# Layer 1 of a two-layer diffusion trunk: high and low weight products in longer groups, down products of two output tiles alternating

## The chip, the cores and the metric

One core of one Trainium2 chip runs the whole program. The metric is the device time of one execution in microseconds (us), the median of several. TensorE (PE) does the matrix products, VectorE (DVE), ScalarE (ACT) and GpSimd (POOL) work elementwise, and SyncE (SP) issues the weight loads.

## The reference

Two layers over 256 latent tokens (and 256 context tokens, which layer 1 only reads) of width 2048. Layer 0 mixes tokens by pooling, layer 1 by neighbourhood attention; each is followed by a gated FFN with a width-3 convolution over tokens. What the change touches is layer 1's output projection and FFN:

```python
D_MODEL, SEQ, D_FF = 2048, 256, 5504

def conv_ffn(u, w_gate, w_up, conv_w, conv_b, w_down):
    T = u.shape[1]
    gp = jnp.pad(u @ w_gate, ((0, 0), (1, 1), (0, 0)))
    gte = gp[:, :T] * conv_w[0] + gp[:, 1:T + 1] * conv_w[1] + gp[:, 2:] * conv_w[2] + conv_b
    return (jax.nn.silu(gte) * (u @ w_up)) @ w_down

# layer i, latent stream
h = h + ml[:, 2] * y_lat              # y_lat of attention ends in o @ w_o
h = h + ml[:, 5] * conv_ffn(modulate(rms_norm(h, norm2_g[i]), ml[:, 3], ml[:, 4]),
                            ffn_w_gate[i], ffn_w_up[i], ffn_conv_w[i], ffn_conv_b[i], ffn_w_down[i])
```

## The kernel before

All products are float32 products made of three shorter ones. A weight tile arrives in pieces of 128 x 1024; `split` (L175, L177) casts each to a high part on ACT, and subtracts it on DVE (of some pieces on POOL) to get the low part. Both parts go into buffers that rotate: six pieces in the FFN, three in the attention. Activations stand as [high | low], 2 x 256 columns. A 512-wide product with the high weight part gives high x high and high x low in the two halves of one PSUM bank; a 256-wide product with the low weight part is added to the second half. They are called high and low products here.

The FFN of layer 1 has 43 tiles of 128 hidden channels, `f`. `gu1(f)` makes a gate tile `g` and an up tile `u`, each over 16 slices `k` of the input: two weight pieces of eight slices. `part` (L1182) does, for one piece, eight high products (L1188) and then eight low ones (L1191), so a tile reads 8 high, 8 low, 8 high, 8 low. `gate1` turns the two banks into one activation tile: `eg` and `eu` join the halves (ACT L1201, DVE L1202), `g1b` is the convolution (ACT L1210, DVE L1211 and L1213), `sgb` the SiLU (ACT L1216) times `eu` (DVE L1217), and `actb` splits that into high and low (ACT L1219, DVE L1220).

Four `f` make a chunk. After the next chunk's tiles, `down1` multiplies a chunk's four activation tiles with 16 output tiles, in four groups `mg` of four (weights `wd_0` to `wd_3` by group). Each output tile takes four high products (L1241) and four low ones (L1245) into one bank; ACT takes the bank out as `dy` (L1255), and POOL adds it to the stream `hl` (L1257) in two halves. Four banks rotate here, so output tile 6 uses the bank of tile 2. There are eleven chunks; the last is done differently and stays so. The gate of the last `f` of the chunk in work is called behind output tile 1 (L1259), so its steps lie at the head of the down phase, among the evictions and the splits of `wd_3`. The o products of the attention (L1614, L1617) follow the scheme of the gate tiles.

A scheduler of the framework fixes, before the run, the order of the instructions on each engine; within an engine they start in that order. The names in a row of the order have counters at the end: `dy_3_2` is chunk 3's eviction of tile 2, `d_3_0_2` is its bank (chunk, group, tile in the group), and `wd_3_3h` is the high part of chunk 3's group 3 (wd_3h in the trace).

Of the kernel before, what the change touches and what calls it, by code (L numbers as in the profile page):

```python
# [17 lines left out]
P = 128  # L18
D = 2048
KT = D // P  # L20
T = 256
# [40 lines left out]
def kernel(ctx: ExitStack, tc: tile.TileContext, xT, cxT, wmod, wg, wu, wd, wp,  # L62
                         wq, wv, wo, vec, cc, rope, inv, strips, out):
    nc = tc.nc
# [8 lines left out]
    def bank(tag, name):  # L73

        if tag == "d" and nbank[0] is not None:
            nbank[0] += 1
            if nbank[0] % 4 == 0:
                tag = "m"
        return pp.tile([P, 512], F32, tag=tag, bufs={"gu": 4, "d": 3, "m": 1}[tag], name=name)

    def flat(a):
        return a.rearrange("p s t -> p (s t)")
# [5 lines left out]
    def V(name):  # L88
        a, b = _OFF[name]
        return vt[0][:, a:b] if b <= NFIRST else vt[1][:, a - NFIRST : b - NFIRST]  # L90
# [72 lines left out]
    def split(ts, name, share=0, keep=False):  # L163

        parts = []
        for j, (t, n) in enumerate(ts):
            turn[0] += 1
            pools = [whp] * 3 + extra
            pool = pools[turn[0] % len(pools)]
            hi = pool.tile([P, 1024], F32R, tag="wh", name=f"{name}h{j}")  # L170
            lo = pool.tile([P, 1024], F32R, tag="wl", name=f"{name}l{j}")
            with ExitStack() as behind:
                for ins in hold:
                    behind.enter_context(tc.issue_after(ins))
                casts.append(nc.scalar.copy(hi[:, :n], t[:, :n]).ins)  # L175
                eng = nc.gpsimd if share and turn[0] % share == 0 else nc.vector
                low_of[:] = [eng.tensor_tensor(lo[:, :n], t[:, :n], hi[:, :n].bitcast(F32), op=ALU.subtract).ins]  # L177
            parts.append((hi, lo))
        if not keep:
            used(ts)  # L180
        return parts

    def ld(src, name, share=0):
        return split(load(lambda a, b: src[:, a:b], 2048, name), name, share)
# [157 lines left out]
    def M(l, which, k, s):  # L342
        return modT[l, which * 4 + k // 4][:, k % 4, s : s + 1]
# [138 lines left out]
    with ExitStack() as ph0:  # L482
# [72 lines left out]
        acts = {}  # L555
# [3 lines left out]
        with ExitStack() as phs:  # L559
# [16 lines left out]
            for j in range(2):  # L576
                t = st.tile([P, 2, WP], F32, bufs=1, name=f"pad{j}")
# [8 lines left out]
            for j in range(2):  # L586
                t = st.tile([P, 4, 32], F32, bufs=1, name=f"sh{j}")
# [239 lines left out]
            for g in range(4):  # L827
# [4 lines left out]
                last = [14]  # L832
# [210 lines left out]
        parts = ld(wv[0, 0], "wv0_0")  # L1043
        normalise_by(h_of, [(k, 0) for k in (2, 3)], rstds, f0, -1)
        last = None
        for kk in range(4):
            for i in range(2):
                ins = first_values(parts, i, kk, last)
                if (kk, i) == (1, 1):
                    with tc.issue_after(ins):  # L1050
                        v1 = n3.sums_of(1)
                    last = n3.done
                if (kk, i) == (2, 1):
                    with tc.issue_after(ins):
                        rstds[1] = n3.spread(1, v1)
                    last = n3.done
# [33 lines left out]
    with ExitStack() as ph2:  # L1090
# [13 lines left out]
        B = {}  # L1104
# [63 lines left out]
        def gu1(f):  # L1168
            if f == 0:
                return first1()  # L1170
            if f == 3:
                hold.clear()
            parts, res = [], []
            for nm, wsrc in (("g", wg), ("u", wu)):
                if f == 1 and nm == "u":
                    hold[:] = [done_b[8][0], done_b[-1][1]]
                parts.append(ahead.pop() if ahead else ld(wsrc[1, f], f"w{nm}1_{f}", 2 if f % 4 > 1 else 0))
                res.append(bank("gu", f"{nm}1_{f}"))
            if f == 1:
                hold[:] = done_b[-1]  # L1180

            def part(q, j):  # L1182

                ps = res[q]
                hi, lo = parts[q][j]
                for k in range(8 * j, 8 * j + 8):
                    c = P * (k % 8)
                    nc.tensor.matmul(ps, hi[:, c : c + P], flat(B[k]), start=(k == 0), stop=False)  # L1188
                for k in range(8 * j, 8 * j + 8):
                    c = P * (k % 8)  # L1190
                    nc.tensor.matmul(ps[:, T:], lo[:, c : c + P], B[k][:, 0], start=False, stop=(k == KT - 1))  # L1191

            for q, j in ((0, 0), (1, 0), (0, 1), (1, 1)) if f == 1 else ((0, 0), (0, 1), (1, 0), (1, 1)):
                part(q, j)
            return res

        def gate1(f, banks):
# [27 lines left out]
        def down1(c, fs, acts, after=None):  # L1225
            n = len(fs)
            last = c == len(chunks) - 1
            for mg in range(4):
                parts = split(load(lambda a, b: wd[1, mg, :, fs[0] + a // 512 : fs[0] + b // 512, :], 512 * n, f"wd1_{c}_{mg}"),
                              f"wd1_{c}_{mg}")  # L1230
                for m in range(4):
                    ps = bank("d", f"d1_{c}_{mg}_{m}")
                    for i in range(n):
                        hi, lo = parts[i // 2]
                        o = 512 * (i % 2) + P * m
                        if last:
                            nc.tensor.matmul(ps[:, :T], hi[:, o : o + P], acts[i][:, 0], start=(i == 0), stop=False)
                            nc.tensor.matmul(ps[:, :T], hi[:, o : o + P], acts[i][:, 1], start=False, stop=False)
                            nc.tensor.matmul(ps[:, :T], lo[:, o : o + P], acts[i][:, 0], start=False, stop=(i == n - 1))
                            continue  # L1240
                        nc.tensor.matmul(ps, hi[:, o : o + P], flat(acts[i]), start=(i == 0), stop=False)  # L1241
                    for i in range(0 if last else n):
                        lo = parts[i // 2][1]
                        o = 512 * (i % 2) + P * m
                        nc.tensor.matmul(ps[:, T:], lo[:, o : o + P], acts[i][:, 0], start=False, stop=(i == n - 1))  # L1245
                    k = 4 * mg + m
                    if last:
                        nc.vector.scalar_tensor_tensor(hl[:, k, :], ps[:, :T], M(1, 5, k, 0), hl[:, k, :],
                                                       op0=ALU.mult, op1=ALU.add)
                        n5.add_stream(h_lat, k, 0, None, (KT - 2, KT - 1))  # L1250
                        for j in {KT - 2: (), KT - 1: (KT - 2, KT - 1)}.get(k, (k,)):
                            nc.scalar.activation(hl[:, j, :], hl[:, j, :], AF.Copy, scale=V("fg")[:, j : j + 1])
                    else:
                        y = f1.tile([P, 2, T], F32, tag="t2", name=f"dy1_{c}_{k}")
                        nc.scalar.activation(flat(y), ps, AF.Copy, scale=M(1, 5, k, 0))  # L1255
                        for q in range(2):
                            nc.gpsimd.tensor_tensor(hl[:, k, :], hl[:, k, :], y[:, q], op=ALU.add)  # L1257
                    if after is not None and 4 * mg + m == 1:
                        after()  # L1259

        prev = None
        for c, fs in enumerate(chunks):
            acts = []
# [45 lines left out]
def _attention(tc, ap0, bank, ld, load, split, used, A, M, hl, wq, wv, wo, rope, strips, ident, v_first, xs, aside, hold):  # L1309

    nc = tc.nc
# [7 lines left out]
    with ExitStack() as es:  # L1319
# [6 lines left out]
        for j in range(2):  # L1326
            t = op.tile([P, 10 * W], F32, name=f"strip{j}")
# [4 lines left out]
        for j in range(2):  # L1332
            t = op.tile([P, 2, T], F32R, name=f"qz{j}")
# [173 lines left out]
        X = {}  # L1507
# [9 lines left out]
        for g in range(4):  # L1517
            v = v_group(g)
            for j in range(4):
                m = 4 * g + j  # L1520
# [38 lines left out]
        for m in range(2):  # L1559
            hold[:] = latest[2] if m else copies  # L1560
            parts = ld(wo[m], f"wo{m}")
            hold.clear()
            ps = bank("gu", f"op{m}")
# [7 lines left out]
        t = third[0][0]  # L1571
# [19 lines left out]
        for m in range(KT):  # L1591
            if m < len(early):
                o_end(early[m][0], m)
                continue
            if m == 3:
                third = load(lambda a, b: wo[3][:, 1024 + a : 1024 + b], 1024, "wo3b")
                parts = [None] + split(third, "wo3b")
                for k in range(8, KT):
                    o_mm(p3, parts, k)
                o_end(p3, m)  # L1600
                continue
            hold[:] = latest[2] if m == 2 else ()
            parts = ld(wo[m], f"wo{m}")
            hold.clear()
            ps = bank("gu", f"op{m}")
            if m == KT - 1:
                for k in range(KT):
                    o_mm(ps, parts, k, True)
            else:
                for j in range(2):  # L1610
                    hi, lo = parts[j]
                    for k in range(8 * j, 8 * j + 8):
                        c = P * (k % 8)
                        nc.tensor.matmul(ps, hi[:, c : c + P], X[k].rearrange("p s t -> p (s t)"), start=(k == 0), stop=False)  # L1614
                    for k in range(8 * j, 8 * j + 8):
                        c = P * (k % 8)
                        nc.tensor.matmul(ps[:, T:], lo[:, c : c + P], X[k][:, 0], start=False, stop=(k == KT - 1))  # L1617
            ins = o_end(ps, m)
        return ins

# [98 lines left out]
```

## Time and profile before

| | us |
|---|---|
| median of 3 runs | 2998.61 (2997.27 to 2998.90) |
| the profiled execution, its own time | 2999.81 |
| its span in the trace | 2998.03 |
| layer 1's FFN in the trace | about 2266 to 2983 |

Every time in a row is counted from the start of the span. In the table of stretches a row has the stretch, its length, and then for PE, PE's weight loads, DVE, ACT and POOL the busy time with the count of instructions, then the granted clock of TensorE, the share of the DMA engines and GB/s. In a timeline "x4" puts four instructions of a kind together from the first start to the last end; the number in brackets is the idle time before the row and what ended it. The granted clock 1.00 stands for 2.4 GHz, 0.50 for 1.2 GHz.

### The profile page before, as it was taken

What the parts mean: (1) busy time and instruction counts of PE and PEld (TensorE: products, weight loads), DVE (VectorE), ACT (ScalarE), POOL (GpSimd) and SP (SyncE); (2) the same over time, 40 slices, a digit from 0 to 9 for tenths busy, and PEclk for the clock granted to TensorE, in tenths of its full rate; (3) what the DMA queues carried; (4) which work ended last, traced back from release to release, by engine and by line L of the source; (5) the groups of instructions that cost most, each with busy time, mean ns of one, the idle gap of its engine ahead of it and who ended that gap; (6) DMA issues with size and microseconds to landing.
All of it is one profiled execution on the core that took longest, in us unless ns stands there. A gap on an engine that the chain in (4) does not pass through costs nothing.

```text
span 2998.0 us, 40831 instructions
## 1 busy us (share of the span) xinstructions
PE 2946.4 (98%) x15068; PEld 2410.7 (80%) x15068; DVE 1989.7 (66%) x2887; ACT 1378.9 (46%) x2239; POOL 808.8 (27%) x782
## 2 busy tenths in 40 slices
PE   5999999999999999999999999999999999999998
PEld 3666678888888888888888888888788888888887
DVE  5465799757484766748576657484868666666666
ACT  4333564333333243332335534353556666666665
POOL 0000006212203031220314002020003665666665
PEclk9999999999999999999999999999999999999999
DMA  9988554566574847557472334343355555555553
GB/s 395 343 314 302 204 180 157 191 202 191 169 230 141 258 138 221 181 177 229 144 252 83 121 107 129 100 131 106 115 166 201 183 190 195 189 183 183 186 193 113
DMA packets 178935, 561.80 MB, mean 187 GB/s; under 512 B 17712, under 2 KB 22576, under 8 KB 178736
## 3 DMA queue, kind: packets, MB, share of 16 engines
q1 hardware_dynamic: 178736, 559.19, 56.2%
q8 instruction: 119, 1.95, 0.2%
q14 instruction: 80, 0.66, 0.1%
HBM read 557.03 MB, written 2.10 MB: 186 GB/s over the span
## 4 chain that ended last, share of the span: by engine, by line
PE 90%; DMA 4%; DVE 3%; POOL 1%; issue 1%; ACT 1%; SPq 0%; DVEq 0%; ACTq 0%; POOLq 0%
PE g L1188 5%; PE u L1188 5%; PE d L971 5%; PE d L969 5%; PE d L970 5%; PE d L1241 5%; PE g L906 4%; PE g L904 4%; PE g L905 4%; PE u L906 4%; PE u L904 4%; PE u L905 4%; PE g L1191 3%; PE u L1191 3%; PE d L1245 2%; PE k L1373 2%
## 5 line engine op out<-in xcount | busy, mean ns | idle before, releaser
L317 DVE SCALAR_TENSOR_TENSOR macc<-wm,sc,macc 128x512 f32<-128x512 f32 (+1 forms) x420 | 379.5, 937 | 70.6 <-DMA wm<-wmod 69.5
L983 POOL TENSOR_TENSOR hl<-hl,dy 128x256 f32<-128x256 f32 x160 | 158.2, 989 | 984.3 <-ACT dy L982 984.2
L1257 POOL TENSOR_TENSOR hl<-hl,dy 128x256 f32<-128x256 f32 x320 | 323.3, 1045 | 214.6 <-ACT dy L1255 212.4
L982 ACT ACTIVATE dy<-d,modT 128x256 f32<-128x256 f32 x320 | 133.4, 470 | 193.0 <-PE d L971 176.4
L983 POOL TENSOR_TENSOR hc<-hc,dy 128x256 f32<-128x256 f32 x160 | 130.7, 817 | 0.0
L1255 ACT ACTIVATE dy<-d,modT 128x512 f32<-128x512 f32 x160 | 104.4, 683 | 43.4 <-PE d L1245 41.9
L177 DVE TENSOR_TENSOR wd_2l<-wd,wd_2h 128x1024 fp32r<-128x1024 f32 (+1 forms) x44 | 56.0, 1277 | 91.3 <-ACT wd_2h L175 90.3
L177 DVE TENSOR_TENSOR wd_3l<-wd,wd_3h 128x1024 fp32r<-128x1024 f32 (+1 forms) x44 | 53.8, 1242 | 79.8 <-ACT wd_3h L175 78.6
L249 PE MATMUL mod<-wm,sc 128*32 128x512 f32 x704 | 86.3, 625 | 6.5 <-DMA wm<-wmod 5.0
L1343 POOL TENSOR_TENSOR rk<-rk,rp 128x256 f32<-128x256 f32 x16 | 12.3, 771 | 296.0 <-DVE rk L1342 296.0
L177 DVE TENSOR_TENSOR wd_1l<-wd,wd_1h 128x1024 fp32r<-128x1024 f32 (+1 forms) x44 | 54.8, 1249 | 48.5 <-ACT wd_1h L175 48.5
L413 POOL TENSOR_TENSOR n2v<-n2v,minus_half 128x4 f32<-128x4 f32 x1 | 1.0, 1012 | 308.8 <-DVE n2v L412 308.8
L175 ACT CAST wd_1h<-wd 128x1024 fp32r<-128x1024 f32 (+1 forms) x44 | 45.3, 1031 | 67.7 <-PE u L905 41.6
L1440 ACT ACTIVATE sb<-sb,nm 128x512 f32<-128x512 f32 x64 | 46.1, 721 | 58.9 <-DVE nm L1436 40.3
L538 ACT ACTIVATE sg<-g 128x512 f32<-128x512 f32 x43 | 27.2, 632 | 99.7 <-DVE g L535 99.7
L177 DVE TENSOR_TENSOR wd_0l<-wd,wd_0h 128x1024 fp32r<-128x1024 f32 (+1 forms) x44 | 54.6, 1246 | 24.9 <-ACT wd_0h L175 24.9
L969 PE MATMUL d<-act,wd_1h 128*128 128x512 f32 x172 | 67.0, 390 | 0.8 <-ACT dy L982 0.8
L969 PE MATMUL d<-act,wd_2h 128*128 128x512 f32 x172 | 67.0, 390 | 0.0
L970 PE MATMUL d<-act,wd_2h 128*128 128x512 f32 x172 | 66.9, 389 | 0.0
L970 PE MATMUL d<-act,wd_1h 128*128 128x512 f32 x172 | 66.9, 389 | 0.0
L969 PE MATMUL d<-act,wd_0h 128*128 128x512 f32 x172 | 66.9, 389 | 0.0
L971 PE MATMUL d<-act,wd_2l 128*128 128x512 f32 x172 | 66.7, 390 | 0.1
(1800 smaller groups left out, 9233.8 us busy)
## 6 DMA issues: line engine op xcount, KB each, us to landing
wm<-wmod SPq DMA_DIRECT2D x384, 512.0 KB, 6.3
wd<-wd SPq DMA_DIRECT2D x168, 512.0 KB, 4.3
wg<-wg SPq DMA_DIRECT2D x156, 512.0 KB, 4.7
wu<-wu SPq DMA_DIRECT2D x156, 512.0 KB, 4.7
wv<-wv SPq DMA_DIRECT2D x32, 512.0 KB, 3.8
wk<-wq SPq DMA_DIRECT2D x32, 512.0 KB, 3.7
wq<-wq SPq DMA_DIRECT2D x32, 512.0 KB, 3.6
wo<-wo SPq DMA_DIRECT2D x31, 512.0 KB, 4.5
```

What stands on the lines that cost most here:

```text
L177: low_of[:] = [eng.tensor_tensor(lo[:, :n], t[:, :n], hi[:, :n].bitcast(F32), op=ALU.subtract).ins]
L317: nc.vector.scalar_tensor_tensor(acc[s], v, sc2[:, k, s : s + 1], acc[s], op0=ALU.mult, op1=ALU.add)
L904: nc.tensor.matmul(ps, hi[:, c : c + P], xh, start=(k == 0), stop=False)
L905: nc.tensor.matmul(ps, hi[:, c : c + P], xl, start=False, stop=False)
L906: ins = nc.tensor.matmul(ps, lo[:, c : c + P], xh, start=False, stop=(k == KT - 1))
L969: nc.tensor.matmul(ps, hi[:, o : o + P], xh, start=(i == 0), stop=False)
L970: nc.tensor.matmul(ps, hi[:, o : o + P], xl, start=False, stop=False)
L971: ins = nc.tensor.matmul(ps, lo[:, o : o + P], xh, start=False, stop=(i == n - 1))
L983: nc.gpsimd.tensor_tensor(h_of(s)[:, k, :], h_of(s)[:, k, :], y[:, s], op=ALU.add)
L1188: nc.tensor.matmul(ps, hi[:, c : c + P], flat(B[k]), start=(k == 0), stop=False)
L1191: nc.tensor.matmul(ps[:, T:], lo[:, c : c + P], B[k][:, 0], start=False, stop=(k == KT - 1))
L1257: nc.gpsimd.tensor_tensor(hl[:, k, :], hl[:, k, :], y[:, q], op=ALU.add)
```

## The change

Three places of layer 1 are written in another order. A gate or up tile does all 16 high products and then all 16 low ones (82 tiles; the tiles of `f` = 0 and 1 stay as they are). The o products of output tiles 6 to 14 do the same (9 tiles). In the first ten chunks the output tiles of the down products go in pairs: four high of one, four high of the next, then the four low of one and the four low of the next, held behind the last high product (80 pairs). The number of instructions and their sizes stay.

```diff
--- before.py
+++ after.py
@@ -1179,19 +1179,19 @@
             if f == 1:
                 hold[:] = done_b[-1]
 
-            def part(q, j):
+            def part(q, js):
 
                 ps = res[q]
-                hi, lo = parts[q][j]
-                for k in range(8 * j, 8 * j + 8):
+                ks = range(8 * js[0], 8 * js[-1] + 8)
+                for k in ks:
                     c = P * (k % 8)
-                    nc.tensor.matmul(ps, hi[:, c : c + P], flat(B[k]), start=(k == 0), stop=False)
-                for k in range(8 * j, 8 * j + 8):
+                    nc.tensor.matmul(ps, parts[q][k // 8][0][:, c : c + P], flat(B[k]), start=(k == 0), stop=False)
+                for k in ks:
                     c = P * (k % 8)
-                    nc.tensor.matmul(ps[:, T:], lo[:, c : c + P], B[k][:, 0], start=False, stop=(k == KT - 1))
-
-            for q, j in ((0, 0), (1, 0), (0, 1), (1, 1)) if f == 1 else ((0, 0), (0, 1), (1, 0), (1, 1)):
-                part(q, j)
+                    nc.tensor.matmul(ps[:, T:], parts[q][k // 8][1][:, c : c + P], B[k][:, 0], start=False, stop=(k == KT - 1))
+
+            for q, js in ((0, (0,)), (1, (0,)), (0, (1,)), (1, (1,))) if f == 1 else ((0, (0, 1)), (1, (0, 1))):
+                part(q, js)
             return res
 
         def gate1(f, banks):
@@ -1228,21 +1228,33 @@
             for mg in range(4):
                 parts = split(load(lambda a, b: wd[1, mg, :, fs[0] + a // 512 : fs[0] + b // 512, :], 512 * n, f"wd1_{c}_{mg}"),
                               f"wd1_{c}_{mg}")
+                pair = {}
                 for m in range(4):
-                    ps = bank("d", f"d1_{c}_{mg}_{m}")
-                    for i in range(n):
+                    if last:
+                        ps = bank("d", f"d1_{c}_{mg}_{m}")
+                    elif m % 2 == 0:
+                        for mm in (m, m + 1):
+                            pair[mm] = bank("d", f"d1_{c}_{mg}_{mm}")
+                            for i in range(n):
+                                o = 512 * (i % 2) + P * mm
+                                high = nc.tensor.matmul(pair[mm], parts[i // 2][0][:, o : o + P], flat(acts[i]),
+                                                        start=(i == 0), stop=False)
+                        for mm in (m, m + 1):
+                            for i in range(n):
+                                o = 512 * (i % 2) + P * mm
+                                with ExitStack() as behind:
+                                    if i == 0:
+                                        behind.enter_context(tc.issue_after(high.ins))
+                                    nc.tensor.matmul(pair[mm][:, T:], parts[i // 2][1][:, o : o + P], acts[i][:, 0],
+                                                     start=False, stop=(i == n - 1))
+                    if not last:
+                        ps = pair[m]
+                    for i in range(n if last else 0):
                         hi, lo = parts[i // 2]
                         o = 512 * (i % 2) + P * m
-                        if last:
-                            nc.tensor.matmul(ps[:, :T], hi[:, o : o + P], acts[i][:, 0], start=(i == 0), stop=False)
-                            nc.tensor.matmul(ps[:, :T], hi[:, o : o + P], acts[i][:, 1], start=False, stop=False)
-                            nc.tensor.matmul(ps[:, :T], lo[:, o : o + P], acts[i][:, 0], start=False, stop=(i == n - 1))
-                            continue
-                        nc.tensor.matmul(ps, hi[:, o : o + P], flat(acts[i]), start=(i == 0), stop=False)
-                    for i in range(0 if last else n):
-                        lo = parts[i // 2][1]
-                        o = 512 * (i % 2) + P * m
-                        nc.tensor.matmul(ps[:, T:], lo[:, o : o + P], acts[i][:, 0], start=False, stop=(i == n - 1))
+                        nc.tensor.matmul(ps[:, :T], hi[:, o : o + P], acts[i][:, 0], start=(i == 0), stop=False)
+                        nc.tensor.matmul(ps[:, :T], hi[:, o : o + P], acts[i][:, 1], start=False, stop=False)
+                        nc.tensor.matmul(ps[:, :T], lo[:, o : o + P], acts[i][:, 0], start=False, stop=(i == n - 1))
                     k = 4 * mg + m
                     if last:
                         nc.vector.scalar_tensor_tensor(hl[:, k, :], ps[:, :T], M(1, 5, k, 0), hl[:, k, :],
@@ -1607,14 +1619,14 @@
                 for k in range(KT):
                     o_mm(ps, parts, k, True)
             else:
-                for j in range(2):
-                    hi, lo = parts[j]
-                    for k in range(8 * j, 8 * j + 8):
+                for js in ((0,), (1,)) if m < 6 else ((0, 1),):
+                    for k in range(8 * js[0], 8 * js[-1] + 8):
                         c = P * (k % 8)
-                        nc.tensor.matmul(ps, hi[:, c : c + P], X[k].rearrange("p s t -> p (s t)"), start=(k == 0), stop=False)
-                    for k in range(8 * j, 8 * j + 8):
+                        nc.tensor.matmul(ps, parts[k // 8][0][:, c : c + P], X[k].rearrange("p s t -> p (s t)"),
+                                         start=(k == 0), stop=False)
+                    for k in range(8 * js[0], 8 * js[-1] + 8):
                         c = P * (k % 8)
-                        nc.tensor.matmul(ps[:, T:], lo[:, c : c + P], X[k][:, 0], start=False, stop=(k == KT - 1))
+                        nc.tensor.matmul(ps[:, T:], parts[k // 8][1][:, c : c + P], X[k][:, 0], start=False, stop=(k == KT - 1))
             ins = o_end(ps, m)
         return ins
 
```

On PE, at the head of chunk 3's down phase, before, from the last high product of output tile 0:

```order
L1241 MATMUL d_3_0_0_21552<-actb_20911,wd_3_0h_21548 128x512
L1245 MATMUL d_3_0_0_21552<-actb_20555,wd_3_0l_21545 128x256
L1245 MATMUL d_3_0_0_21552<-actb_20661,wd_3_0l_21545 128x256
L1245 MATMUL d_3_0_0_21552<-actb_20767,wd_3_0l_21549 128x256
L1245 MATMUL d_3_0_0_21552<-actb_20911,wd_3_0l_21549 128x256
L1241 MATMUL d_3_0_1_21565<-actb_20555,wd_3_0h_21544 128x512
```

The same place in the changed kernel, where the high product is L1240 and the low one L1248:

```order
L1240 MATMUL d_3_0_0_21552<-actb_20911,wd_3_0h_21548 128x512
L1240 MATMUL d_3_0_1_21557<-actb_20555,wd_3_0h_21544 128x512
L1240 MATMUL d_3_0_1_21557<-actb_20661,wd_3_0h_21544 128x512
L1240 MATMUL d_3_0_1_21557<-actb_20767,wd_3_0h_21548 128x512
L1240 MATMUL d_3_0_1_21557<-actb_20911,wd_3_0h_21548 128x512
L1248 MATMUL d_3_0_0_21552<-actb_20555,wd_3_0l_21545 128x256
```

Four high products of tile 1 moved in front of the low products of tile 0.

The scheduler also moved instructions of other engines. ACT, the same down phase, before:

```order
L1255 ACTIVATE dy_3_1_21574<-d_3_0_1_21565,modT_20_11884 128x512
L1201 COPY eg_21578<-g_19_21462 128x256
L1201 COPY eu_21581<-u_19_21475 128x256
L1210 ACTIVATE g1b_21584<-eg_21578,vt_71 128x256
L175 CAST wd_3_3h_21752<-wd_3_3_0_21748 128x1024
L175 CAST wd_3_3h_21756<-wd_3_3_1024_21750 128x1024
L1216 ACTIVATE sgb_21588<-g1b_21584 128x256
L1255 ACTIVATE dy_3_2_21603<-d_3_0_2_21594,modT_20_11884 128x512
```

And ACT in the changed kernel:

```order
L1267 ACTIVATE dy_3_1_21574<-d_3_0_1_21557,modT_20_11884 128x512
L1201 COPY eg_21578<-g_19_21462 128x256
L1201 COPY eu_21581<-u_19_21475 128x256
L175 CAST wd_3_3h_21752<-wd_3_3_0_21748 128x1024
L1210 ACTIVATE g1b_21584<-eg_21578,vt_71 128x256
L175 CAST wd_3_3h_21756<-wd_3_3_1024_21750 128x1024
L1216 ACTIVATE sgb_21588<-g1b_21584 128x256
L1267 ACTIVATE dy_3_2_21612<-d_3_0_2_21594,modT_20_11884 128x512
```

The first cast of wd_3 and `g1b` changed places; `sgb` still stands before the eviction of tile 2, and those of tiles 3 to 5 follow it.

DVE at the same place, before:

```order
L1202 TENSOR_TENSOR eu_21581<-eu_21581,u_19_21475 128x256
L1211 SCALAR_TENSOR_TENSOR g1b_21584<-eg_21578,vt_71,g1b_21584 128x255
L1213 SCALAR_TENSOR_TENSOR g1b_21584<-eg_21578,vt_71,g1b_21584 128x255
L177 TENSOR_TENSOR wd_3_3l_21753<-wd_3_3_0_21748,wd_3_3h_21752 128x1024
L177 TENSOR_TENSOR wd_3_3l_21757<-wd_3_3_1024_21750,wd_3_3h_21756 128x1024
L1217 TENSOR_TENSOR sgb_21588<-sgb_21588,eu_21581 128x256
```

And DVE in the changed kernel:

```order
L1202 TENSOR_TENSOR eu_21581<-eu_21581,u_19_21475 128x256
L177 TENSOR_TENSOR wd_3_3l_21753<-wd_3_3_0_21748,wd_3_3h_21752 128x1024
L1211 SCALAR_TENSOR_TENSOR g1b_21584<-eg_21578,vt_71,g1b_21584 128x255
L177 TENSOR_TENSOR wd_3_3l_21757<-wd_3_3_1024_21750,wd_3_3h_21756 128x1024
L1213 SCALAR_TENSOR_TENSOR g1b_21584<-eg_21578,vt_71,g1b_21584 128x255
L1217 TENSOR_TENSOR sgb_21588<-sgb_21588,eu_21581 128x256
```

The two subtractions of wd_3 moved in front of the two convolution steps of `g1b`, one before each. The other nine down phases read the same on ACT and DVE.

## Rows read from the trace of the kernel before

**Rows 1.** The page: busy us of each engine, with its share of the span.

```profile
PE 2946.4 (98%) x15068; PEld 2410.7 (80%) x15068; DVE 1989.7 (66%) x2887; ACT 1378.9 (46%) x2239; POOL 808.8 (27%) x782
```

**Rows 2.** Stretches of layer 1's FFN: us, then busy us of each engine, clock.

```profile
2340.00:2943.00 603.00, 603.00 (x3452) 529.45 (x3451) 405.91 (x397) 371.23 (x538) 382.56 (x322) 1.00 0.57 188
2943.00:2982.80 39.80, 39.80 (x274) 36.97 (x274) 28.48 (x43) 30.32 (x58) 30.17 (x32) 1.00 0.19 60
```

**Rows 3.** The chain of waits, one gate tile: start us, us, what.

```profile
2294.41 1.84 PE g L1188 x8
2296.25 0.95 PE g L1191 x8
```

**Rows 4.** Timeline, PE: first and last product of long runs of one width.

```profile
1006.99 0.40 PE L904 MATMUL g<-A,wg_26h 128*128 128x512 f32 x1
...
1016.54 0.39 PE L904 MATMUL g<-A,wg_26h 128*128 128x512 f32 x1
...
2252.90 0.28 PE L1539 MATMUL op<-A,wo15h 128*128 128x256 f32 x1
...
2258.30 0.28 PE L1539 MATMUL op<-A,wo15h 128*128 128x256 f32 x1
```

**Rows 5.** Tile wg_20h, 2561 to 2580: shortest/median/longest ns, first and last start.

```profile
L1188 PE MATMUL g<-A,wg_20h x16: 387/395/398, 2567.0 to 2578.4; 128*128 128x512 f32 x16
L175 ACT CAST wg_20h<-wg x2: 1039/1044/1050, 2562.1 to 2563.1; 128x1024 fp32r<-128x1024 f32 x2
```

**Rows 6.** Timeline, head of chunk 3's down products (start us, us, engine, line).

```profile
2551.53 1.09 PE L1241 MATMUL d<-actb,wd_0h 128*128 128x512 f32 x4
...
2553.13 0.69 ACT L1255 ACTIVATE dy<-d,modT 128x512 f32<-128x512 f32 x1 [1.30 <-PE d L1245]
...
2554.54 0.69 ACT L1255 ACTIVATE dy<-d,modT 128x512 f32<-128x512 f32 x1 [0.72 <-PE d L1245]
...
2555.12 0.36 ACT L1201 COPY eg<-g 128x256 f32<-128x256 f32 x1
...
2555.37 0.39 ACT L1201 COPY eu<-u 128x256 f32<-128x256 f32 x1
...
2555.97 0.60 ACT L1210 ACTIVATE g1b<-eg,vt 128x256 f32<-128x256 f32 x1 [0.21 <-DVE eg L1202]
...
2556.48 1.99 ACT L175 CAST wd_3h<-wd 128x1024 fp32r<-128x1024 f32 x2
2556.61 0.65 DVE L1211 SCALAR_TENSOR_TENSOR g1b<-eg,vt,g1b 128x255 f32<-128x255 f32 x1 [0.34 <-ACT g1b L1210]
...
2557.30 0.48 DVE L1213 SCALAR_TENSOR_TENSOR g1b<-eg,vt,g1b 128x255 f32<-128x255 f32 x1
2557.70 2.35 DVE L177 TENSOR_TENSOR wd_3l<-wd,wd_3h 128x1024 fp32r<-128x1024 f32 x2
...
2558.37 0.42 ACT L1216 ACTIVATE sgb<-g1b 128x256 f32<-128x256 f32 x1
...
2558.69 2.40 ACT L1255 ACTIVATE dy<-d,modT 128x512 f32<-128x512 f32 x4
...
2559.95 1.09 PE L1241 MATMUL d<-actb,wd_1h 128*128 128x512 f32 x4
```

**Rows 7.** Timeline, the same place in chunk 8: third eviction and tile 6.

```profile
2894.39 2.39 ACT L1255 ACTIVATE dy<-d,modT 128x512 f32<-128x512 f32 x4
...
2895.65 1.09 PE L1241 MATMUL d<-actb,wd_1h 128*128 128x512 f32 x4
```

**Rows 8.** Groups by line, VectorE (DVE), 2340 to 2943: busy us, mean ns.

```profile
L1213 DVE SCALAR_TENSOR_TENSOR g1b<-eg,vt,g1b 128x255 f32<-128x255 f32 x36 | 37.8, 1049 | 1.3
...
L177 DVE TENSOR_TENSOR wd_3l<-wd,wd_3h 128x1024 fp32r<-128x1024 f32 x18 | 21.2, 1219 | 0.0
```

**Rows 9.** Two other stretches where PE pauses, with their granted clock (PEclk).

```profile
42.90:46.30 3.40, 2.64 (x16) 0.68 (x16) 3.03 (x7) 2.01 (x5) 0.00 (x0) 0.50 1.03 411
...
2262.00:2266.00 4.00, 3.52 (x25) 2.93 (x24) 2.33 (x5) 0.64 (x1) 3.17 (x3) 1.00 0.63 184
```

## The prediction

> **What bounds the kernel now.** I read the busy shares first: TensorE (PE) works 98% of the span, VectorE (DVE) 66%, ScalarE (ACT) 46% [rows 1]. A share is an average, so the stretch that the change touches comes next. In layer 1's FFN PE is busy 603.00 of 603.00 us, then 39.80 of 39.80, at a granted clock of 1.00 [rows 2]. Every product there starts as the one before it lets it, and nothing that another engine does shows in the end. So two things can move the time: the pace of PE through a reordered row of products, and a new moment at which another engine is too late for it. For the first I read PE's pace in runs of one width [rows 3, 4], for the second the handover of one down phase, engine by engine [rows 6]. The profiled execution took 2999.81 us, 1.20 above the median of 2998.61; differences are worked out inside the trace and put on the median.
>
> **PE's pace: a small gain.** Instruction counts stay. A gate or up tile is now 8 high products in 1.84 us, 8 low in 0.95, and both again [rows 3], 5.58 in all. Without a change of width a high product follows the last at (1016.54 - 1006.99)/42 = 0.2274 us, and a 256-wide one at (2258.30 - 2252.90)/45 = 0.1200 us (42 and 45 products of one width lie between the rows) [rows 4]. So 16 high take 1.84 + 8 x 0.2274 = 3.66, 16 low 0.95 + 8 x 0.12 = 1.91, together 5.57: 0.01 us less. That is 91 tiles (82 gate and up tiles, 9 o products), -0.9 us. A down tile takes (2559.95 - 2551.53)/6 = 1.403 us [rows 6]; a pair was 2.81 and becomes 1.403 + 4 x 0.2274 + 4 x 0.12 = 2.79, -0.014 each, and 80 pairs give -1.1. Sum **-2.0 us**; the starts are rounded to 0.01 us, so I keep 0 to -4. The same run of 256-wide products excludes that a longer row of low products starves on its weight loads: it holds 0.1200 over 45 [rows 4].
>
> A rule speaks against even this gain. The rows show that the change of width costs a little: 1.84/8 = 0.230 against 0.2274 [rows 3, 4]. The Trainium skill ("TensorE: Matmul & The Clock Gate", section "Back-to-back issue gap") gives the gap of an isolated product from its own width alone, N/2.4 + 2.5 ns, which is 215.8 ns at 512 and 109.2 at 256. By it the order of widths is worth nothing, and the sum would lose its -2.0. The trace is about 11 ns slower at either width, so I keep the rows.
>
> **The weights: nothing.** The second half's high weights are now wanted 8 low products, 0.95 us, sooner. For wg_20 the last cast starts at 2563.1 and takes 1.05, while the tile's first product is at 2567.0 [rows 5]: the second half is there before the first half is used, so 0.95 us of it costs nothing. The low half is wanted later. Loads and their queue only swap neighbours.
>
> **The down phase: a new wait.** The low products of tile 0 now stand behind the high ones of tile 1, so tile 0 is complete later, and its eviction `dy_0` with it. Before, it started 2553.13, that is 1.60 after tile 0 [rows 6]. Now four high products (4 x 0.2274 = 0.91) come between: 2554.04. Evictions follow each other at (2.40 - 0.69)/3 = 0.57 [rows 6], so `dy_1` starts 2554.61, and `eg`, which came 0.58 behind `dy_1` (2555.12 - 2554.54), starts 2555.19, `eu` 2555.44 [rows 6]. This would be harmless, since tile 4 wants the bank of tile 0 only at 2557.1. The order of the three engines decides. Next on ACT now stands the first cast of wd_3 (before, `g1b`), and on DVE its subtraction (L177) stands before the first `g1b` step (L1211), the second subtraction before the second step (L1213). Before, both steps stood in front of both subtractions. ACT's `sgb` needs L1213, and `dy_2` to `dy_5` are queued behind `sgb`. So PE's bank for tile 6, the one of tile 2, now waits for two weight subtractions.
>
> Worked out for chunk 3:
> - The first cast needs the buffer that tile 3's second high product frees. Before, the cast came 2556.48, with tile 3 started at 2551.53 + 3 x 1.403 = 2555.74, so 0.74 after [rows 6]. Tile 3's high products now start one pair and four high later, 2551.53 + 2.79 + 0.92 = 2555.24, so the cast may start between 2555.8 (ACT free) and 2556.0, and ends about 2556.9 (1.99 for two).
> - The subtraction follows at about 2557.0; it takes 2.35/2 = 1.17: 2558.15.
> - L1211 took 0.65, its twin L1213 let the next start after 0.40 (2557.70 - 2557.30); between them about 0.5: 2558.65. The second subtraction, 1.17: 2559.8. L1213, 0.48 [rows 6]: 2560.3.
> - `sgb` then lets `dy_2` go 0.32 later (2558.69 - 2558.37) and `dy_2` takes 0.69 [rows 6]: done 2561.3, and the high products of tile 6 start about 2561.4.
> - PE is there after three pairs, 2551.53 + 3 x 2.79 = 2559.90.
>
> So PE stands 1.5 us. Before, `dy_2` was done at 2559.38 and tile 6 began at 2559.95 [rows 6], a margin of 0.57; in chunk 8 the same two starts lie 1.26 apart, as in chunk 3 [rows 7]. The new order stands at the head of all ten phases. **10 x 1.5 = +15.0 us.** Bounds: with every step at its shortest (cast done 2556.8, subtraction 1.12, L1211 0.40) 1.1 us. With DVE slowed as it is on average beside GpSimd (POOL), whose adds of `dy_0` and `dy_1` run at the same time, subtractions take 1.22 and L1213 1.05 [rows 8], and it is 2.3 us. I take 1.5, since at this place L1213 took 0.48 and not the mean. What is late next is `dy_3`, 0.57 behind `dy_2`, done 2561.9; its tile 7 starts its high products 0.92 after tile 6, at 2562.3: 0.4 to spare. Tile 8 needs `dy_4`, done 2562.5, at 2564.2. The stall is not won back, as PE has no idle time after it.
>
> Sum: 2998.61 + 15.0 - 2.0 = **3011.6 us** (in the profiled execution's terms 2999.81 + 13.0 = 3012.8).
>
> **Rivals.**
> - No stall: `dy_2` is in time, because the subtractions or `sgb` come 1.5 us earlier than worked out. For it: PE has waited for no eviction so far [rows 2]. Against: each step of the chain has a row, and the bound from the short side is 1.1. It is decided by whether `dy_2` is done at 2559.90. Time: 2998.61 - 2.0 = 2996.6, not measurable.
> - A part of it: 0.2 to 0.7 us a phase, 2998.6 to 3003.6; this would need the cast to start well ahead of 2555.8.
> - A second stall behind the first: `dy_3`, or POOL's adds that free the eviction buffers, late by 0.5 us more a phase. Margin 0.4 on `dy_3`. Time 3016.6.
> - The clock falls after each pause. In 42.90 to 46.30 PE paused and ran at 0.50, in 2262 to 2266 it paused for 0.48 us and kept 1.00 [rows 9]. If each of ten pauses cost a stretch such as the first at half pace, 3.4/2 = 1.7 us each: 3011.6 + 17 = 3028.6. The Trainium skill (the same page, "A second HAM failure mode: psum-queue depth-cycling") tells of a kernel whose short pauses between groups, as it cycles through PSUM banks, made the clock swing between both levels. No row here shows that in this stretch.
> - Faster by more than 0.2%: the changes of width cost three times what the rows give, and there is no stall. Against it, the rows of pace.
>
> **How the numbers follow.** A measurement of this kernel tells about 0.2%, 6 us, from no change. The forecast (stall of 1.1 to 2.3 us a phase, with -4 to 0 of pace: 3005.6 to 3021.6) gets 0.68; the second stall 0.08; the clock 0.04; no stall 0.13; the part of it 0.05; faster 0.02. The lowest edge of the forecast and the partial stall overlap near 3004.6, where "same" ends, and 3 in 100 of the forecast fall there by a short first cast: same 0.13 + 0.04 + 0.03 = 0.20, slower 0.78, faster 0.02. The range, 3000 to 3022, holds the forecast, most of the second stall and part of the partial one, 0.79.
>
> **What would show it.** Right: ten waits of PE in layer 1 of about 1.5 us each, at the first high product of the third tile of wd_1, ended by ACT's `dy`; before it ACT's `sgb` waiting for L1213, and on DVE subtraction, L1211, subtraction, L1213 in that order. 16 high products in 3.66 us and 16 low in 1.91 show the pace right. Wrong: PE again busy all of 603 us, then the handover was mis-timed and the change is worth its 2 us of pace; a granted clock under 1.00 in the stretch means the last slow rival; PE waits at other tiles mean a second stall.

## The result and the profile after

| | before, us | changed, us |
|---|---|---|
| median of 5 runs | 2998.90 (2997.27 to 3000.48) | 3019.34 (3015.94 to 3024.73) |
| ratio, 95% interval | | 1.0068 (1.0057 to 1.0078) |
| span of the profiled execution | 2998.03 | 3017.6 |

The changed kernel is 20.4 us slower; the forecast was 13.0 slower, 3011.6, with a range to 3022. PE's busy time on the page (beside [rows 1]) is nearly what it was:

```profile
PE 2947.9 (98%) x15068; PEld 2415.1 (80%) x15068; DVE 1979.5 (66%) x2887; ACT 1380.2 (46%) x2239; POOL 789.0 (26%) x782
```

So PE did the same work, and the 19.6 us of span are mostly time in which it stood. The waits of PE in layer 1's FFN (us in total, times, longest), where the kernel before had none:

```profile
PE d L1240 <- ACT dy L1267: 17.4, 10, 1.7
```

The pace of a gate tile, from the chain of waits (beside [rows 3]): 16 high products in 3.65 us and 16 low in 1.91, 5.56 where it was 5.58:

```profile
2293.88 3.65 PE g L1188 x16
2297.53 1.91 PE g L1191 x16
```

The timeline of chunk 3's down phase, in the order of time (start us, us, engine, line), beside [rows 6]. Its first product starts at 2556.00 here and at 2551.53 before, so 4.47 is to be taken off to compare:

```profile
2556.00 2.00 PE L1240 MATMUL d<-actb,wd_0h 128*128 128x512 f32 x8
...
2558.51 1.27 ACT L1267 ACTIVATE dy<-d,modT 128x512 f32<-128x512 f32 x2 [3.18 <-PE d L1248]
...
2559.28 2.85 POOL L1269 TENSOR_TENSOR hl<-hl,dy 128x256 f32<-128x256 f32 x4 [17.57 <-ACT dy L1267]
2559.67 0.38 ACT L1201 COPY eg<-g 128x256 f32<-128x256 f32 x1
...
2560.38 1.05 ACT L175 CAST wd_3h<-wd 128x1024 fp32r<-128x1024 f32 x1
...
2561.33 0.60 ACT L1210 ACTIVATE g1b<-eg,vt 128x256 f32<-128x256 f32 x1
...
2561.60 1.61 DVE L177 TENSOR_TENSOR wd_3l<-wd,wd_3h 128x1024 fp32r<-128x1024 f32 x1 [0.78 <-ACT wd_3h L175]
...
2563.14 0.47 DVE L1211 SCALAR_TENSOR_TENSOR g1b<-eg,vt,g1b 128x255 f32<-128x255 f32 x1
...
2563.53 1.21 DVE L177 TENSOR_TENSOR wd_3l<-wd,wd_3h 128x1024 fp32r<-128x1024 f32 x1
2564.67 0.47 DVE L1213 SCALAR_TENSOR_TENSOR g1b<-eg,vt,g1b 128x255 f32<-128x255 f32 x1
2565.23 0.42 ACT L1216 ACTIVATE sgb<-g1b 128x256 f32<-128x256 f32 x1 [2.36 <-DVE g1b L1213]
2565.55 2.41 ACT L1267 ACTIVATE dy<-d,modT 128x512 f32<-128x512 f32 x4
...
2566.28 2.11 PE L1240 MATMUL d<-actb,wd_1h 128*128 128x512 f32 x8 [1.74 <-ACT dy L1267]
```

Read it down to the last row: PE waits 1.74 us for ACT's `dy`; the four evictions start at 2565.55, right behind `sgb` (L1216); `sgb` waited 2.36 us for DVE; and on DVE a subtraction (L177) stands before each of the two `g1b` steps (L1211, L1213).

One thing in the profile was not in the forecast's sum. Of the stretch of ten chunks the granted clock is 0.99 and not 1.00, and in chunk 5 it is 0.50 for a while after the wait (stretch, its length, busy us of PE, its weight loads, DVE, ACT and POOL, then the clock):

```profile
2340.00:2960.00 620.00, 604.32 (x3441) 531.41 (x3439) 394.64 (x395) 371.44 (x537) 363.63 (x322) 0.99 0.55 183
2699.30:2701.20 1.90, 1.90 (x11) 1.57 (x10) 1.86 (x2) 1.30 (x2) 0.57 (x1) 1.00 0.16 60
2705.00:2706.00 1.00, 1.00 (x3) 0.71 (x3) 0.00 (x0) 0.98 (x3) 1.00 (x2) 0.50 0.31 123
2706.00:2708.00 2.00, 2.00 (x9) 1.80 (x8) 0.44 (x1) 1.75 (x2) 2.00 (x4) 0.50 0.09 35
2708.00:2710.00 2.00, 2.00 (x11) 1.74 (x11) 1.56 (x1) 1.41 (x3) 2.00 (x3) 0.92 0.00 0
```

The high products behind that wait, eight in a row, then take 3.05 us, where those of chunk 3 took 2.11:

```profile
2704.01 3.05 PE L1240 MATMUL d<-actb,wd_1h 128*128 128x512 f32 x8 [1.74 <-ACT dy L1267]
```

The tiles' starts in the two traces give the whole account of the profiled execution. From the last low product before tile 6 to tile 6 lie 2.02 us in every phase, 0.12 without a wait: a delay of 1.90, times ten 19.0. The pair behind it takes 2.90 and not 2.79, ten times 0.11: 1.1. In two phases (chunks 5 and 8) that pair takes 4.45, 1.55 more for the clock: 3.1. Against it stands the pace, 0.0175 us for each of 91 tiles and 80 pairs, as the two kernels without waits below show it: -3.0. That is +20.2. The FFN began 0.5 earlier, 0.2 of it the o tiles' gain that is counted already, and the part behind the last down product took 0.4 less. So +19.5 is left, of 19.6 seen.

### The profile page after: what moved, and what is told of

Read it like the earlier page. It is cut to its first block, busy times and chain, and to the rows that moved or that the text cites. A ratio compares the mean times of both kernels' runs of the same rounds, so it can differ in the third digit from the quotient of the medians.

```text
span 3017.6 us, 40823 instructions
## 1 busy us (share of the span) xinstructions
PE 2947.9 (98%) x15068; PEld 2415.1 (80%) x15068; DVE 1979.5 (66%) x2887; ACT 1380.2 (46%) x2239; POOL 789.0 (26%) x782
## 4 chain that ended last, share of the span: by engine, by line
PE 89%; DVE 4%; DMA 3%; issue 2%; ACT 1%; SPq 1%; POOL 0%; DVEq 0%; ACTq 0%; POOLq 0%
PE g L1188 5%; PE u L1188 5%; PE d L971 5%; PE d L969 5%; PE d L970 5%; PE d L1240 4%; PE g L906 4%; PE g L904 4%; PE g L905 4%; PE u L904 4%; PE u L906 4%; PE u L905 4%; PE u L1191 3%; PE g L1191 3%; PE k L1385 2%; PE q L1404 2%
## 5 line engine op out<-in xcount | busy, mean ns | idle before, releaser
L983 POOL TENSOR_TENSOR hl<-hl,dy 128x256 f32<-128x256 f32 x160 | 158.4, 990 | 983.8 <-ACT dy L982 983.6
L1269 POOL TENSOR_TENSOR hl<-hl,dy 128x256 f32<-128x256 f32 x320 | 307.0, 997 | 224.6 <-ACT dy L1267 224.6
L177 DVE TENSOR_TENSOR wd_3l<-wd,wd_3h 128x1024 fp32r<-128x1024 f32 (+1 forms) x44 | 59.2, 1345 | 88.7 <-ACT wd_3h L175 87.6
L177 DVE TENSOR_TENSOR wd_2l<-wd,wd_2h 128x1024 fp32r<-128x1024 f32 (+1 forms) x44 | 54.9, 1270 | 92.5 <-ACT wd_2h L175 66.5
L177 DVE TENSOR_TENSOR wd_1l<-wd,wd_1h 128x1024 fp32r<-128x1024 f32 (+1 forms) x44 | 54.3, 1237 | 42.2 <-ACT wd_1h L175 33.7
L177 DVE TENSOR_TENSOR wd_0l<-wd,wd_0h 128x1024 fp32r<-128x1024 f32 (+1 forms) x44 | 53.3, 1234 | 34.1 <-ACT wd_0h L175 23.2
```

What stands on the lines that cost most here:

```text
L983: nc.gpsimd.tensor_tensor(h_of(s)[:, k, :], h_of(s)[:, k, :], y[:, s], op=ALU.add)
```

## The experiments

Theory: the two subtractions ahead of the second `g1b` step are the loss. Rivals: the alternation alone makes the evictions late; the longer groups of the gate tiles have a part in it; the price is that of a restart of PE or of its clock, and not of the wait.

**The gate and o part alone, and the down part alone.** The first kernel keeps the new `part` and o loops with the down loop of before; against the changed kernel:

```diff
...
-                    if not last:
-                        ps = pair[m]
-                    for i in range(n if last else 0):
+                    ps = bank("d", f"d1_{c}_{mg}_{m}")
+                    for i in range(n):
...
```

The second does the reverse:

```diff
...
-            for q, js in ((0, (0,)), (1, (0,)), (0, (1,)), (1, (1,))) if f == 1 else ((0, (0, 1)), (1, (0, 1))):
-                part(q, js)
+            for q, j in ((0, 0), (1, 0), (0, 1), (1, 1)) if f == 1 else ((0, 0), (0, 1), (1, 0), (1, 1)):
+                part(q, j)
...
```

> Only the 16 high, 16 low order of the gate, up and o tiles; down products as in the kernel before, and ACT and DVE at the head of a down phase in the order of before. Theory (the loss is the wait in the down phase, the pace gains 0.02 us a tile as the changed kernel's trace shows from tile to tile): no wait of PE in layer 1's FFN, 91 tiles x 0.02 = -1.8 us, 2997.1. Rival (a product's spacing goes by its own width alone): 2998.9, no difference. Second rival (the longer groups want the weights too early): waits of PE on casts, slower than before.

Measured: 2997.22 us, ratio 0.9996 (0.9987 to 1.0005), which by time alone can't be told from no change. The trace tells it: PE is busy through the whole stretch (columns as above),

```profile
2266.00:2940.00 674.00, 674.00 (x3868) 593.38 (x3867) 458.14 (x476) 421.94 (x617) 401.77 (x334) 1.00 0.58 190
```

and between the second tile of `f` = 0 and the last up tile, with 81 changed tiles between them, it gains 1.42 us on the kernel before, 0.0175 a tile. The gap worked out from width alone would give none.

> Only the alternating down products; gate, up and o tiles as in the kernel before. Theory: the whole loss is here, ten waits of 1.74 us on the eviction of tile 2 and about +18.5 us without any fall of the clock, 3017.4; with falls of the clock of 1.6 us each after two or three of the ten waits 3019 to 3022. Rival (the longer gate and up groups make part of the loss): under 3012.

Measured: 3019.74 us, ratio 1.0070 (1.0057 to 1.0083). All ten waits are here, 1.73 us each:

```profile
PE d L1240 <- ACT dy L1267: 17.3, 10, 1.7
```

Two of them (chunks 3 and 5) were followed by slow products, the pair behind them taking 4.47 and 4.45 us where the other eight take 2.90. So the loss is all in the down part, and the rival on the longer groups falls.

**Alternating products, with the order of before on ACT and DVE.** `gated` holds ACT's `g1b` (L1210) and DVE's second step (L1213), and `hold` makes a split issue behind them, each part on its engine:

```diff
...
+            gated.append(second.ins)
...
+                if mg == 3 and not last:
+                    hold[:] = gated
+                parts = split(staged, f"wd1_{c}_{mg}")
+                if mg == 3 and not last:
+                    hold.clear()
```

> The changed kernel with all its products, but the cast of wd_3 held behind ACT's g1b, and its subtraction behind DVE's second g1b step, so that ACT and DVE have the order of before. Theory (the two subtractions in front of the g1b steps are the cause): dy_2 is done 0.3 us before PE wants its bank, no wait of PE there, and only the pace is left, 91 x 0.02 + 80 x 0.02 = -3.4 us, 2995.5. Rival (the alternation alone makes the chain late, since dy_0 comes 0.9 us later): a wait of 0.3 to 1 us stays in each of the ten phases, 2999 to 3006.

Measured: 2995.79 us, ratio 0.9988 (0.9980 to 0.9997): no wait is left, and the kernel is faster than both. Its stretch and the head of chunk 3 (here the `g1b` steps are L1213 and L1215, `sgb` L1219, `dy` L1274, high products L1247):

```profile
2266.00:2940.00 674.00, 674.00 (x3873) 594.86 (x3872) 508.45 (x480) 415.92 (x621) 398.29 (x336) 1.00 0.58 190
```

```profile
2554.99 0.54 DVE L1213 SCALAR_TENSOR_TENSOR g1b<-eg,vt,g1b 128x255 f32<-128x255 f32 x1 [0.34 <-ACT g1b L1212]
...
2555.56 0.86 DVE L1215 SCALAR_TENSOR_TENSOR g1b<-eg,vt,g1b 128x255 f32<-128x255 f32 x1
2556.34 2.35 DVE L177 TENSOR_TENSOR wd_3l<-wd,wd_3h 128x1024 fp32r<-128x1024 f32 x2
2556.76 0.41 ACT L1219 ACTIVATE sgb<-g1b 128x256 f32<-128x256 f32 x1
...
2557.07 2.40 ACT L1274 ACTIVATE dy<-d,modT 128x512 f32<-128x512 f32 x4
...
2558.20 2.00 PE L1247 MATMUL d<-actb,wd_1h 128*128 128x512 f32 x8
```

Both `g1b` steps run before the subtractions, `sgb` starts at 2556.76, and `dy_2`, 0.67 us long here, is done at 2557.74, 0.47 before tile 6 starts at 2558.20 (0.59 in the kernel before, by the same reading). The alternation itself leaves enough room; it is the order on DVE and ACT that costs. From the first down product of one chunk to that of the next lie 66.86 us here and 67.00 in the kernel with the gate and o part alone: 0.14 for eight pairs, 0.0175 a pair.

**The gate behind output tile 15.** One number:

```diff
-                    if after is not None and 4 * mg + m == 1:
+                    if after is not None and 4 * mg + m == 15:
```

> The changed kernel, but the gate of the chunk's last tile is called behind output tile 15 and not behind tile 1, so no step of it stands among the first evictions. Theory: dy_2 goes as soon as its products are done, over 2 us ahead of PE, no wait in the down phase, -3.4 us, 2995.5. Rival (the gate's steps only move the wait to the next chunk's tiles, where the splits of wg and wu stand): new waits of PE on casts or evictions there, 2998 or more.

Measured: 3003.06 us, ratio 1.0014 (1.0005 to 1.0023). The waits in the ten phases are gone as the theory says, but one new one of 5.8 us stands before the last chunk:

```profile
PE d L1255 <- ACT actb L1219: 5.8, 1, 5.8
```

The last chunk's down products follow directly on the tenth phase, and now need the activation tile of a gate that was just called. The rival was right that a wait comes up elsewhere, though at one place and not at each chunk's tiles. Without it, the start of the last up tile (f = 42) stands 2.6 us earlier than in the kernel before when the start of the FFN is set equal, and 2.7 earlier in the kernel with the gate's steps first. From that start to the last down product it then takes 7.6 us more than that kernel, 5.8 for the wait and 1.8 for what follows: during the wait the granted clock fell to 0.50, and the first products behind it ran at that level (columns as above):

```profile
2966.80:2970.00 3.20, 0.00 (x0) 0.00 (x1) 2.73 (x4) 0.82 (x2) 3.20 (x3) 0.50 0.00 0
2970.00:2973.50 3.50, 3.50 (x16) 3.50 (x17) 2.22 (x6) 1.23 (x4) 2.37 (x4) 0.50 0.00 0
```

**One subtraction instead of two.** As above, but only the second piece of wd_3 is held:

```diff
...
+                    parts = split(staged[:1], nm)
+                    hold[:] = gated
+                    parts = parts + split(staged[1:], nm + "b")
+                    hold.clear()
...
```

> The changed kernel, but only the first subtraction of wd_3 stands in front of DVE's g1b steps; the second is held behind them. Theory (the wait is the DVE time put ahead of the second g1b step): one subtraction of 1.14 us less on the chain, so 0.6 to 0.7 us of wait in each phase instead of 1.74, ten of them, and about 11.4 us less than the changed kernel: 3005 (from 3016.2 without falls of the clock). Rival (any wait there costs the same by a restart of PE): over 3012. On the clock: if its falls come from the length of a wait, none is seen here.

Measured: 3006.21 us, ratio 1.0024 (1.0014 to 1.0034), ten waits of 0.73 us:

```profile
PE d L1250 <- ACT dy L1277: 7.3, 10, 0.7
```

Against the changed kernel the wait fell by 1.0 us, one subtraction on the chain. The products behind it take 2.90 us in all ten phases: no slow clock in this profile.

**Both subtractions ahead, without alternation.** The kernel before, with repeated maxima of `g1b` with itself between the two steps, two (`late`) in the gates of the down phases:

```diff
...
+            for _ in range(late):
+                nc.vector.tensor_tensor(g1, g1, g1, op=ALU.max)
...
```

> The kernel before, no alternation, 8 and 8 groups; in the ten gates of the down phases two repeated 256-wide maxima of g1b with itself (0.4 us each, the values stay) stand between DVE's two g1b steps, and the order then has both subtractions of wd_3 in front of the second step. Theory (two subtractions ahead of L1213 are enough, with or without alternation): dy_2 is done at 2561.8 where tile 6 was at 2559.95, a delay of 1.9 us in each of ten phases, 1.75 of it shown as a wait, 3018 and falls of the clock on top. Rival (the loss needs the alternating products): under 3003.

Measured: 3018.26 us, ratio 1.0063 (1.0050 to 1.0076). DVE's rows at chunk 3 (the maximum is L1214, the second step L1215), and the waits:

```profile
2562.20 0.63 DVE L1211 SCALAR_TENSOR_TENSOR g1b<-eg,vt,g1b 128x255 f32<-128x255 f32 x1 [0.34 <-ACT g1b L1210]
...
2562.87 0.42 DVE L1214 TENSOR_TENSOR g1b<-g1b 128x256 f32<-128x256 f32 x1
2563.21 1.22 DVE L177 TENSOR_TENSOR wd_3l<-wd,wd_3h 128x1024 fp32r<-128x1024 f32 x1
...
2564.34 0.42 DVE L1214 TENSOR_TENSOR g1b<-g1b 128x256 f32<-128x256 f32 x1
...
2564.68 1.22 DVE L177 TENSOR_TENSOR wd_3l<-wd,wd_3h 128x1024 fp32r<-128x1024 f32 x1
...
2565.82 0.48 DVE L1215 SCALAR_TENSOR_TENSOR g1b<-eg,vt,g1b 128x255 f32<-128x255 f32 x1
```

```profile
PE d L1243 <- ACT dy L1257: 17.4, 10, 1.8
```

The same ten waits of 1.74 us, with products in the old order. So the alternation is not needed for the loss; it only led the scheduler to the order that makes it. In the rows above the two maxima take up 0.34 us each of the way from the first step to the second, and the two subtractions 1.13 and 1.14, so most of the delay is theirs. That the wait comes out as in the changed kernel, to 0.01 us, is chance: there the evictions before it start 0.9 us later and no maxima stand in the way.

**The clock: the changed kernel again, and one with a longer wait.** The first is the changed kernel, for a second profile. The second has five such maxima before the second `g1b` step.

> The changed kernel once more, for a second profile. The first had a granted clock of 0.50 for some 3 us after two of its ten waits, each 1.6 us. If these falls come by chance after a pause, the profile shows another number or other phases, with the same ten waits of 1.74 us, and times spread in steps of 1.6 us from about 3016. If they belong to fixed places, they stand again at the down phases of chunks 5 and 8.

Measured: 3017.42 us (3014.87 to 3020.20), ratio 1.0061 (1.0047 to 1.0075). The same ten waits, and a clock of 1.00 in the stretch, with a pair of 2.90 behind every one:

```profile
PE d L1240 <- ACT dy L1267: 17.3, 10, 1.7
```

```profile
2340.00:2960.00 620.00, 604.39 (x3459) 531.72 (x3458) 393.09 (x398) 374.73 (x539) 370.53 (x322) 1.00 0.56 184
```

So the slow products are not bound to a place: two phases in one profile, none in the other. That the spread of the times comes in steps of 1.6 us can't be seen in them, since the kernel before spreads by 4 us as well.

> The changed kernel with five repeated 256-wide maxima of g1b with itself (0.40 to 0.43 us each, the values stay) in front of DVE's second g1b step in the ten gates of the down phases. Theory: each wait grows from 1.74 by 2.0 to 2.2 to about 3.8 us, +21 us without the clock, 3037. On the clock: if a longer pause makes a fall likelier, most of the ten phases show 0.50 after it, up to 1.6 us more each, 3050; if the falls do not depend on the length, two or three, 3041.

Measured: 3058.78 us (3058.47 to 3059.74), ratio 1.0198 (1.0184 to 1.0212), and a wait of 4.0 us in each phase:

```profile
PE d L1242 <- ACT dy L1269: 40.3, 10, 4.0
```

The stretch has a clock of 0.97, and after the first wait, which ends at 2362.48, PE starts at 0.50 (columns as above):

```profile
2340.00:3000.00 660.00, 623.72 (x3466) 547.18 (x3465) 411.99 (x443) 372.47 (x537) 361.54 (x322) 0.97 0.53 173
2362.50:2363.50 1.00, 1.00 (x3) 0.81 (x4) 0.00 (x0) 1.00 (x3) 1.00 (x2) 0.50 0.03 8
2363.50:2366.00 2.50, 2.50 (x7) 1.98 (x6) 0.43 (x1) 1.51 (x4) 2.50 (x4) 0.50 0.02 7
2366.00:2370.00 4.00, 4.00 (x18) 3.52 (x17) 2.37 (x2) 2.71 (x4) 4.00 (x6) 0.68 0.00 0
```

In all ten phases the pair behind the wait takes 4.2 to 5.3 us and not 2.9. The wait alone explains 10 x (4.03 - 1.74) = 23 us over the changed kernel, and the time rose by 39 to 41 over the two medians of it. The rest, some 17 us, is what the clock cost beyond its falls in those two: the starts of the chunks' tiles give about 20 us for the ten falls of this profile. The forecast's upper case, 3050, was still too low, since one fall cost 1.3 to 2.8 us here.

## Why the prediction was right, and where its size was off

- **What bounds the kernel, and where the wait comes.** Right. Ten waits at the third tile of wd_1, ended by `dy`, with `sgb` waiting for L1213 and the subtractions in front: as written before the run, to the tile.
- **The chain, term by term.** With 4.47 taken off, `dy_0` started at 2554.04 (forecast 2554.04), the cast at 2555.91 (2555.8 to 2556.0), the first subtraction at 2557.13 (2557.0). It then took 1.61 us, not 1.17, and L1211 came at 2558.67 and not at 2558.15. This is the term that was mis-sized. All later steps keep that 0.4 to 0.5: L1213 at 2560.20 (2559.8), `sgb` 2560.76 (2560.3), `dy_2` 2561.08 (2560.6), tile 6 2561.81 (2561.4). The delay was 1.90 and not 1.5, 4 us over ten phases.
- **Why the first subtraction was longer.** When it started, POOL was still at its adds of `dy_0` and `dy_1` (2559.28 to 2562.13); the subtraction ended at 2563.21, 1.08 behind them. The second one, with POOL idle, took 1.21, and in the kernel with the old order of products both took 1.22 (its rows above). The same stands wherever a long POOL instruction was in progress, as in these two rows of the changed kernel, which end at 2328.86 and 2329.94:

```profile
2326.45 2.41 POOL L177 TENSOR_TENSOR wg_7l<-wg,wg_7h 128x1024 fp32r<-128x1024 f32 x1 [3.16 <-ACT wg_7h L175]
...
2327.37 2.57 DVE L177 TENSOR_TENSOR wg_7l<-wg,wg_7h 128x1024 fp32r<-128x1024 f32 x1 [2.33 <-ACT wg_7h L175]
```

In the ten traces, from the splits of wg_3 on, 899 of the 128x1024 subtractions on DVE started with more than 0.2 us of a POOL instruction still to run, and 898 of them ended 1.07 to 1.10 us behind it; the 981 that met no POOL instruction took 1.21 to 1.23. So POOL's adds held the subtraction back by about 0.4 us. No run moved POOL's adds away from this place, but the agreement leaves little room for another cause. The forecast had named DVE beside POOL as its upper bound and then taken the undisturbed value because L1213 was undisturbed at that place; but the instruction that now met POOL's adds was another. That 1.90 lay inside the bounds is in part luck: the upper one came from 1.05 for L1213, which took 0.47, and from 1.22 for a subtraction, which is its length without POOL. The Trainium skill ("SBUF — State Buffer", section "SBUF: two separate sides") tells of a pair of ports that VectorE and GpSimd share as a lock: the one that starts first holds it for its whole instruction, an operation of VectorE with two inputs in SBUF, such as a subtraction, among them, and the other waits. The 1.08 us behind POOL's end agrees with it.

- **The restart.** Not in the forecast: the pair behind each wait takes 2.90 and not 2.79, 1.1 us in all.
- **The clock.** A rival with 4 in 100, put as a fall in all ten phases. It came in two of ten in the profiled execution, 1.55 us each, 3.1 us. The forecast asked whether a pause brings it always or never; the runs show that it depends on the pause: none of ten after waits of 0.73 us, four of forty after waits of 1.74 (four profiles), ten of ten after 4.0, and the one of 5.8. The rule of the Trainium skill on short pauses between groups ("TensorE: Matmul & The Clock Gate", section "A second HAM failure mode: psum-queue depth-cycling") held in part: the clock did swing here, in a kernel that cycles through four banks, though only after four of forty waits of 1.74 us and after none of 0.73.
- **The pace.** Right in its small size: 0.0175 a tile where 0.01 was forecast, and as much a pair where 0.014 was. The rule by width alone, which gave no gain, is not borne out by 16 high products in 3.65 us against 2 x 1.84 [rows 3].
- **No stall, a second stall.** Neither came: `dy_3` was in time in every phase, as PE waited once in each.

Sum: 15.0 became 19.0, the restart added 1.1 and the clock 3.1, the pace gave 3.0 and not 2.0.

What stays open: why a wait of 1.74 us brings the slow clock in some phases and not in others, and what makes the 0.1 us of the restart.

## What to carry to other kernels

When a scheduler sets the order, compare the order on every engine, not only on the one whose code was changed: here a harmless edit on PE let two weight subtractions slip in front of a step that evictions stand behind, and holding the subtractions back took the changed kernel from 3019.3 to 2995.8 us. An eviction queued behind an activation that waits for another engine is the place to look first, with the margin between its end and the next use of its bank (0.59 us before, 0.47 in the best kernel). And a chain should be priced with what will run beside each of its instructions in the new place, not with what ran beside it in the old one.

## What the runs showed of the hardware

- A tile of 16 high and 16 low products cost 0.0175 us less when they stood as 16 and 16 and not as 8, 8, 8 and 8, which is two changes of width fewer: about 0.01 us for each.
- A pause of PE has a price beyond its length: about 0.1 us at the restart in each of the 46 waits of 0.73 and 1.74 us (of 50) that no slow clock followed, and after the other four a granted clock of 0.50 for some 3 us, 1.55 us lost each; after each of ten waits of 4.0 us that clock, with 1.3 to 2.8 us lost, and after the one of 5.8 us, with 1.8 lost.
- A 128x1024 float32 subtraction on DVE that started while a POOL instruction was running ended 1.08 us behind that instruction (898 of 899 cases with more than 0.2 us of it left), so it took 1.61 us at the place that matters here; with no POOL instruction beside it, it took 1.21 to 1.23.
